# Modulation weights loaded in tiles of 512 columns, and two modulation steps moved from the second expert stage into the second mixer

## The chip, the cores and the metric

The kernel runs on one core of one Trainium2 chip. The core has five engines that run their own instruction streams: TensorE (PE in the profile; its weight loads are listed apart as PEld), VectorE (DVE), ScalarE (ACT), GpSimd (POOL) and SyncE (SP), which here only issues transfers. Sixteen DMA engines move data between device memory and the core's on-chip memory. The metric is the time of one execution on the device, in microseconds.

## The reference

A diffusion-transformer block of two layers over 256 latent tokens and 256 context tokens, width 1024, batch 1, all in float32. Each layer has a mixer and a mixture of experts, and both are modulated by vectors that are made from the conditioning vectors c (for the latent tokens) and c_ctx (for the context):

```python
mod_lat = jnp.split((jax.nn.silu(c) @ w_mod[l] + b_mod[l])[:, None, :], 6, axis=-1)
mod_ctx = jnp.split(jax.nn.silu(c_ctx) @ w_mod[l] + b_mod[l], 6, axis=-1)
u_lat = to_scan_order(rms_norm(h_lat, norm1_g[l]) * (1 + mod_lat[1]) + mod_lat[0], rows, l)
...
z_lat = jnp.split(u_lat @ w_in[l], split_at, axis=-1)
...
y_lat = from_scan_order(jnp.concatenate([a_lat, m_lat, r_lat], axis=-1) @ w_out[l], rows, l)
h_lat = h_lat + mod_lat[2] * y_lat
v_lat = rms_norm(h_lat, norm2_g[l]) * (1 + mod_lat[4]) + mod_lat[3]
h_lat = h_lat + mod_lat[5] * hier_moe(v_lat, *moe_p)
```

`w_mod[l]` is 1024 x 6144. The mixer (`a`, `m`, `r`) is a gated convolution of 31 taps, a chunked mLSTM with four heads in two directions, and a gated linear recurrence. `hier_moe` routes each token to 2 of 16 experts (width 512; three matrices of 1024 x 512 each). In the last layer only the latent tokens go through the convolution, the output projection and the experts. The result is a final RMS norm of the latent tokens.

## The kernel before

The program runs mixer, experts, mixer, experts. PE's order is the order in which the code is written (a manual schedule for PE); the orders of ACT, DVE, POOL and SP and the use of the buffers are chosen by the framework's scheduler, from the dependences and its own model of the program.

**Modulation.** The 6144 columns of a layer are worked off in twelve steps q = 0 to 11 of 512 columns (two steps to one of the six vectors). A step loads its 2 MB of `w_mod` as two tiles (`wcols`, L209 to L210, whose transfers are recorded at L187). `mod_mm` (L219 to L230) multiplies them with `cS`, the silu of both conditioning vectors, spread over groups of 32 output partitions (L225), and copies the sum to `mp` (L228, ACT). `mod_fin` transposes `mp` four times on PE (L234), adds the four partial sums on DVE (L236) and the bias (L238), into `modc`. Whoever needs a vector reads `modc`. Between the two halves of a step the next one may start: `pump` places `mod_mm` of the next step and then `mod_fin` of the one before it, on PE behind the place where it is called. In the mixers these places have names (`site("k1")` and so on), and the table `SITES` says at which of them a step is placed; `pump(100)` at the end of the mixer's heads takes what is left. In the expert stages `pump(2)` is called twice ahead of the routing, and again at places of the last expert of the first layer.

**Where the steps stand.** Layer 1's first six steps are done in the first expert stage, steps 6 to 9 in the second mixer at k1, v3, g0 and o0, and steps 10 and 11 at the start of the second expert stage. Steps 10 and 11 make `mod_lat[5]`, which `gate_rows` reads when the fourth expert of the order is worked off (`OVER`).

**Buffers.** A ring of seven tiles of 1 MB holds weights of `w_in`, `w_out` and `w_mod`, and in the expert stages also expert weights. A tile of `w_in` or `w_out` is split into a high and a low part (`wsplit`): ACT casts the high part (L191), DVE and POOL each subtract one half of it from the raw tile (L192), so that it takes three tiles of the ring. Expert weights (`ahead`, `ewt`; transfers at L1122 and L1128) go into fifteen buffers in turn: B, three pairs of q4 halves, uLa, uLb, the ring, uTa and uTb. Most of these are also buffers of the second mixer, and a load waits until the mixer has given its buffer back. SP issues all loads in one order.

**The second mixer.** After the projections of q, k, v (L517) the mLSTM goes through its chunks (`chunk_b`); in a chunk PE multiplies `X`, the masked and scaled scores, with the values (L837) and the scaled queries `qs` with the state (L839). DVE makes `X` in steps (L813, L814, L822), POOL makes `qs` (L821), and DVE reads the normaliser `dn` (L840) and adds the heads' outputs into `hacc` (L865). The convolution's norm (L911 to L931) and the recurrence's gate `g` (POOL L953, L954; DVE L955, L957) run beside it. Then come the two tiles of the output gate (`o_tile`, L517, with two tiles of `w_in`, the o-weights), the heads' norm (L985 to L998), and `w_out` (L1050).

**The start of the second expert stage.** Behind `w_out` DVE makes `xs`, the normalised tokens (L275); PE transposes them (L283) and multiplies with the router's weights (L331); DVE makes the routing from the logits (L1177 to L1311, `m`); PE then sorts (L1218 to L1259), and the first expert's gate and up projections begin (L1356).

Of the kernel before, what the change touches and what calls it, by code (L numbers as in the profile page):

```python
# [14 lines left out]
P = 128  # L15
D = 1024
KC = 8
# [10 lines left out]
NPE = 1  # L28
BP = (2, 3)

SITES = ("q0 q1 k0 v3 v1 o0 o1", "k1 v3 g0 o0")
PV = ((1, 1), (1, 1))
START = {mybir.EngineType.Activation, mybir.EngineType.DVE, mybir.EngineType.Pool, mybir.EngineType.SP}
LOE = ((0, 1), (0, 1), (0, 1), (0, 1))
# [5 lines left out]
def hybrid_kernel(ctx, tc, x, c, cx, c_ctx, w_mod, b_mod, norm1_g, norm2_g, w_in, conv_w, conv_b, conv_ln_g,  # L40
# [4 lines left out]
    V, S, G, T = nc.vector, nc.scalar, nc.gpsimd, nc.tensor  # L45
# [13 lines left out]
    def bank(shape=(P, 512)):  # L59
        cnt[0] += 1  # L60
        return box["ps"].tile(list(shape), F32, tag="ps", name=f"ps{cnt[0]}", bufs=box["nps"])

    def kt(shape, dt=F32, name=None, tag=None, bufs=1):
        return keep.tile(list(shape), dt, name=name, tag=tag or name, bufs=bufs)
# [68 lines left out]
    cS = kt([P, KC, 32], name="cS")  # L133
# [50 lines left out]
    def wtile(src, shape, pool=None):  # L184
        wn[0] += 1
        t = (pool or ring).tile(list(shape), F32, tag="w", name=f"w{wn[0]}")
        nc.sync.dma_start(t, src)  # L187
        return t
# [20 lines left out]
    def wcols(w, a, n=256):  # L209
        return wtile(w[:, a:a + n].rearrange("(k p) f -> p k f", p=P), [P, KC, n])  # L210


    def mod_ld(l, q, between=None):
        a = wcols(w_mod[l], q * 512)
        if between:
            between()
        return [a, wcols(w_mod[l], q * 512 + 256)]

    def mod_mm(l, q, tmp, ws=None):  # L219
        ps = bank()  # L220
        for hf in range(2):
            w = ws[hf] if ws else wcols(w_mod[l], q * 512 + hf * 256)
            for k in range(KC):
                j = k % 4
                T.matmul(ps[32 * j:32 * j + 32, hf * 256:hf * 256 + 256], cS[:, k, :], w[:, k, :],  # L225
                         start=(k < 4), stop=(k >= 4))
        mp = tmp.tile([P, 512], F32, tag="t2", name=f"mp{l}_{q}")
        S.copy(mp, ps)  # L228
        return mp
# [10 lines left out]
    def mod_pair(l, q, tmp):  # L240
        mod_fin(l, q, mod_mm(l, q, tmp))
# [108 lines left out]
    def mixer(l, hs, fill):  # L350
# [5 lines left out]
        with tc.tile_pool(name=f"mx{l}", bufs=1, reuse_waits="tile") as mx, \  # L356
# [23 lines left out]
            def pump(n=1):  # L380
                for _ in range(n):
                    late = box.pop("late", None)
                    if fill:
                        box["late"] = fill.pop(0)(tmp)
                    if late:
                        late()

            def site(name):
                pump(SITES[l].split().count(name))

# [15 lines left out]
            if l == 0:  # L406
# [8 lines left out]
                warm = sm("warm", [P, 1])  # L415
                S.activation(warm, onec, AF.Silu)
                mw = {0: mod_ld(0, 0)}
                xin = [hload(x, "xl", "hl"), hload(cx, "xc", "B")]
                mw[2] = mod_ld(0, 2)
                w16 = thin_w()  # L420

# [7 lines left out]
                for q in (1, 3):  # L429
                    mw[q] = mod_ld(0, q)  # L430
# [36 lines left out]
                def warm_up(n):  # L467

                    for _ in range(n):
                        T.matmul(wps[:, 0:P], ident, ident, start=True, stop=True)  # L470

                mp0 = mod_mm(0, 0, tmp, mw[0])
                columns(1)
                mod_fin(0, 0, mp0)
# [3 lines left out]
                into(1)  # L478
                turn((0, 1))
                mp2 = mod_mm(0, 2, tmp, mw[2])  # L480
                warm_up(3)
                w0 = [wx[1:]]
# [1240 lines left out]
    def mod_late(l, q, tmp):  # L1723
        mp = mod_mm(l, q, tmp)

        def fin():
            mod_fin(l, q, mp)
            if (l, q) == (1, 3):
                mod_scale(s1, 1, 1, "n1")
        return fin  # L1730

    mods = [[(lambda tmp, l=l, q=q: mod_late(l, q, tmp)) for q in range(12)] for l in range(2)]
    with tc.manual_schedule(engines={mybir.EngineType.PE}):
        hs = mixer(0, None, mods[0][4:])
        hs = moe(0, hs, mods[1][:4 + len(BP)])
        hs = mixer(1, hs, mods[1][4 + len(BP):10])
        moe(1, hs, mods[1][10:])


_INS = ['x', 'c', 'ctx', 'c_ctx', 'w_mod', 'b_mod', 'norm1_g', 'norm2_g', 'w_in', 'conv_w', 'conv_b', 'conv_ln_g',  # L1740
# [49 lines left out]
```

## Time and profile before

| | |
|---|---|
| median of 3 runs | 1188.36 us (1186.65 to 1193.46) |
| profiled execution | 1189.1 us, its span 1187.5 us |
| busy share of the span | PE 88%, DVE 46%, ACT 31%, POOL 19% |
| moved by DMA | 313.19 MB, mean 264 GB/s |
| loads of w_mod | 48 of 1024 KB, median 6.8 us from issue to landing |

The span is the time from the first to the last instruction of the profiled execution; the whole execution takes a little longer. All times of single instructions are counted from the start of the span. A matmul of the program appears as two or more records in the trace. The names of the ring's tiles are left out in the trace (`w`), while the split tiles keep theirs (`w238h` for a high part, `w238l` for a low part).

### The profile page before, as it was taken

The numbers are of one execution on the slowest core, as the hardware profiler recorded it, in microseconds if no ns is written. First come the engines' busy times: TensorE is split into PE (matmuls) and PEld (weight loads), VectorE is DVE, ScalarE is ACT, GpSimd is POOL, SyncE is SP. The second block draws the span as 40 slices with busy tenths as digits, with TensorE's granted clock in tenths as the row PEclk, the third lists the DMA queues.
The fourth block names the chain that finished last, engine by engine and source line by source line (L and its number), as shares of the span: only waits on it lengthen the run. The fifth ranks groups of instructions, "written<-read, shape, count | busy, mean of one in ns | idle before, by whom it ended". The sixth has DMA issues, their size and how long they took to land. (4 is left out here: it accounts for less than half of the span.)

```text
span 1187.5 us, 21557 instructions
## 1 busy us (share of the span) xinstructions
PE 1040.2 (88%) x8655; PEld 718.5 (61%) x8655; DVE 541.1 (46%) x1239; ACT 363.4 (31%) x713; POOL 227.7 (19%) x241
## 2 busy tenths in 40 slices
PE   6989989999989979999999678989887887888966
PEld 4667778899764535445453356769786564455532
DVE  3779977762451111120101789974775211012115
ACT  3545254443331111111111344644442221122202
POOL 3412123414100000000000634111441000000112
PEclk9999989999999989999999889989998998999998
DMA  9735743376878877898887633442679899999981
GB/s 314 228 106 169 258 145 96 107 252 245 261 312 336 324 256 310 308 369 333 341 324 289 217 120 109 142 142 95 222 271 381 330 411 412 412 406 412 412 317 54
DMA packets 144009, 313.19 MB, mean 264 GB/s; under 512 B 26116, under 2 KB 108336, under 8 KB 124032
## 3 DMA queue, kind: packets, MB, share of 16 engines
q1 hardware_dynamic: 128896, 295.74, 67.4%
q0 software_dynamic: 14704, 14.92, 3.9%
q8 instruction: 102, 1.67, 0.6%
q10 hardware_dynamic: 272, 0.57, 0.1%
q14 instruction: 35, 0.29, 0.1%
HBM read 298.25 MB, written 20.71 MB: 269 GB/s over the span
## 5 line engine op out<-in xcount | busy, mean ns | idle before, releaser
L1391 DVE TENSOR_TENSOR hT<-sg,ps 128x256 f32<-128x256 f32 x63 | 24.9, 421 | 319.7 <-ACT sg L1382 319.3
L1356 PE MATMUL X<-w,XT 128*32 128x256 f32 (+1 forms) x2016 | 138.1, 398 | 22.9 <-PEq L1647 6.4
L1472 POOL DMA_DIRECT2D Yd<-Y x90 | 33.4, 386 | 518.9 <-ACT Y L1468 462.8
L1356 PEld LDWEIGHTS X<-w,XT 128*32 128x32 f32 (+1 forms) x2016 | 75.7, 113 | 84.1 <-issue 38.4
L1356 PE MATMUL ps<-w,XT 128*64 128x512 f32 x512 | 115.9, 605 | 11.3 <-PEq L1478 5.9
L1242 PE MATMUL ps<-P,vh 128*128 128x256 f32 x336 | 87.7, 297 | 9.5 <-PEq L1611 8.1
L1356 PEld LDWEIGHTS ps<-w,XT 128*64 128x64 f32 x512 | 42.9, 139 | 80.5 <-issue 64.7
L1242 PE MATMUL ps<-P,vl 128*128 128x256 f32 x336 | 82.7, 282 | 0.0
L756 DVE SCALAR_TENSOR_TENSOR acc<-cb,cwh,acc 128x512 f32<-128x512 f32 (+1 forms) x120 | 80.1, 706 | 1.0
L1242 PEld LDWEIGHTS ps<-P,vh 128*128 128x128 f32 x336 | 64.2, 191 | 24.5 <-issue 12.1
L1373 ACT COPY gs<-X 128x512 f32<-128x512 f32 x45 | 26.3, 586 | 169.3 <-PEq L1611 55.5
L1468 DVE COPY Y<-Y 128x512 f32<-128x512 f32 x30 | 20.8, 692 | 98.3 <-PEq L1647 29.4
L1404 PE MATMUL Y<-w,hT 128*32 128x256 f32 (+1 forms) x912 | 59.7, 387 | 5.6 <-issue 4.0
L1242 PEld LDWEIGHTS ps<-P,vl 128*128 128x128 f32 x336 | 64.3, 191 | 0.0
L225 PE MATMUL ps<-w,cS 128*32 128x256 f32 x768 | 49.6, 397 | 10.1 <-DMA w<-in_w_mod_dram 9.7
L1404 PE MATMUL ps<-w,hT 128*64 128x512 f32 x240 | 54.8, 598 | 0.3 <-DVE hT L1391 0.2
L1379 PE MATMUL ps<-blob,gs 128*128 128x128 f32 x256 | 42.0, 290 | 10.8 <-PEq L1624 3.4
L1404 PEld LDWEIGHTS Y<-w,hT 128*32 128x32 f32 (+1 forms) x912 | 28.7, 111 | 33.6 <-issue 14.7
L1373 ACT COPY gs<-ps 128x512 f32<-128x512 f32 x15 | 8.8, 587 | 123.6 <-PE ps L1356 123.6
L1379 PEld LDWEIGHTS ps<-blob,gs 128*128 128x128 f32 x256 | 27.7, 144 | 26.7 <-issue 15.5
L225 PEld LDWEIGHTS ps<-w,cS 128*32 128x32 f32 x768 | 22.7, 113 | 31.1 <-DMA w<-in_w_mod_dram 11.0
L1382 ACT ACTIVATE sg<-ps 128x256 f32<-128x256 f32 x64 | 24.2, 391 | 43.4 <-PE ps L1379 26.8
(893 smaller groups left out, 2083.3 us busy)
## 6 DMA issues: line engine op xcount, KB each, us to landing
w<-in_w_down_dram SPq DMA_DIRECT2D x58, 1024.0 KB, 13.0
w<-in_w_gate_dram SPq DMA_DIRECT2D x49, 1024.0 KB, 11.3
w<-in_w_mod_dram SPq DMA_DIRECT2D x48, 1024.0 KB, 6.8
w<-in_w_up_dram SPq DMA_DIRECT2D x48, 1024.0 KB, 12.2
w<-in_w_in_dram SPq DMA_DIRECT2D x23, 1024.0 KB, 6.6
w<-in_w_up_dram SPq DMA_DIRECT2D x32, 512.0 KB, 9.1
w<-in_w_gate_dram SPq DMA_DIRECT2D x30, 512.0 KB, 10.0
w<-in_w_out_dram SPq DMA_DIRECT2D x8, 1024.0 KB, 5.5
```

The costliest lines, as they stand in the source:

```text
L225: T.matmul(ps[32 * j:32 * j + 32, hf * 256:hf * 256 + 256], cS[:, k, :], w[:, k, :], start=(k < 4), stop=(k >= 4))
L756: V.scalar_tensor_tensor(acc[:, ch], src, wcol, acc[:, ch], op0=OP.mult, op1=OP.add)
L1242: T.matmul(ps[:, cc, :], v[:, i, k * P:k * P + P], P2[:, i, :], start=(n == 0), stop=(n == 2 * NT - 1))
L1356: T.matmul(ps[w * t:w * t + w, o0:o0 + q], XT[:, k, c0:c0 + w], ws[2 * g + k // 4][k % 4][:, f0:f0 + q], start=(k == 0), stop=(k == KC - 1))
L1373: S.copy(o, src)
L1379: T.transpose(pt[:, f, :], gs[:, f * P:f * P + P], ident)
L1382: S.activation(sg, pt[:, :, 0:64], AF.Silu)
L1391: V.tensor_tensor(hT, sg, pt[:, :, 64:128], op=OP.mult)
L1404: T.matmul(ps[w * t:w * t + w, o0:o0 + q], hk, ws[4 + k // 2][k % 2][:, q * t:q * t + q], start=(k == 0), stop=(k == 3))
L1468: (V.tensor_copy if b else S.copy)(Y, ps)
L1472: nc.gpsimd.dma_start(Yd[x, s0:s0 + w, :].rearrange("s (h f) -> h s f", f=q), Y[:, q * c:q * c + q], **({"cond": n_s > s0} if s0 else {}))
```

## The change

Each load of a modulation step takes 512 rows and all of the step's 512 columns, where before it took all 1024 rows and 256 columns; the tile is 128 x 4 x 512 instead of 128 x 8 x 256. A step's matmuls have 512 columns and there are eight instead of sixteen. `SITES[1]` has two more places, v2 and g1; the second mixer is given steps 6 to 11, and the second expert stage none. Behind the edited functions line numbers fall by 3 or 4.

```diff
-SITES = ("q0 q1 k0 v3 v1 o0 o1", "k1 v3 g0 o0")
+SITES = ("q0 q1 k0 v3 v1 o0 o1", "k1 v2 v3 g0 g1 o0")
...
-    def mod_ld(l, q, between=None):
-        a = wcols(w_mod[l], q * 512)
-        if between:
-            between()
-        return [a, wcols(w_mod[l], q * 512 + 256)]
+    def mod_ld(l, q):
+        return [wtile(w_mod[l][512 * h:512 * h + 512, q * 512:q * 512 + 512].rearrange("(k p) f -> p k f", p=P),
+                      [P, 4, 512]) for h in range(2)]
 
     def mod_mm(l, q, tmp, ws=None):
         ps = bank()
-        for hf in range(2):
-            w = ws[hf] if ws else wcols(w_mod[l], q * 512 + hf * 256)
-            for k in range(KC):
-                j = k % 4
-                T.matmul(ps[32 * j:32 * j + 32, hf * 256:hf * 256 + 256], cS[:, k, :], w[:, k, :],
-                         start=(k < 4), stop=(k >= 4))
+        ws = ws or mod_ld(l, q)
+        for k in range(KC):
+            j = k % 4
+            T.matmul(ps[32 * j:32 * j + 32, :], cS[:, k, :], ws[k // 4][:, j, :], start=(k < 4), stop=(k >= 4))
...
-        hs = mixer(1, hs, mods[1][4 + len(BP):10])
-        moe(1, hs, mods[1][10:])
+        hs = mixer(1, hs, mods[1][4 + len(BP):])
+        moe(1, hs, [])
```

On SP, in the second mixer, before (the last two `w_in` tiles are the o-weights; 128x1024 are halves of expert weights in q4 buffers):

```order
L187 DMA w_8991<-in_w_mod_dram 128x8x256
L1128 DMA w_9713<-in_w_gate_dram 128x2048
L187 DMA w_9001<-in_w_mod_dram 128x8x256
L187 DMA w_9168<-in_w_in_dram 128x8x256
L187 DMA w_9176<-in_w_in_dram 128x8x256
L1122 DMA w_9715<-in_w_up_dram 128x1024
L187 DMA w_9318<-in_w_mod_dram 128x8x256
L187 DMA w_9328<-in_w_mod_dram 128x8x256
L187 DMA w_9446<-in_w_out_dram 128x8x256
```

And the same place after the change:

```order
L187 DMA w_8853<-in_w_mod_dram 128x4x512
L1124 DMA w_9581<-in_w_gate_dram 128x2048
L187 DMA w_8855<-in_w_mod_dram 128x4x512
L187 DMA w_9023<-in_w_mod_dram 128x4x512
L187 DMA w_9025<-in_w_mod_dram 128x4x512
L187 DMA w_9044<-in_w_in_dram 128x8x256
L1118 DMA w_9583<-in_w_up_dram 128x1024
L1118 DMA w_9584<-in_w_up_dram 128x1024
L1118 DMA w_9587<-in_w_gate_dram 128x1024
L1118 DMA w_9588<-in_w_gate_dram 128x1024
L187 DMA w_9052<-in_w_in_dram 128x8x256
```

One more step's tiles stand ahead of the o-weights, and four halves of expert weights now stand between the two o-weights.

On DVE, at the last chunk of the mLSTM, before (`w240l` is the low part of the second o-weight, `X` and `dn` belong to the chunk, `g` to the recurrence's gate, `xnat` to the convolution's norm):

```order
L822 TENSOR_TENSOR X_9080<-X_9080,st_1_8827 128x512
L814 TENSOR_TENSOR X_9080<-X_9080,blob 128x512
L916 BN_AGGR bag_8942<-bst_8941 128x2
L192 TENSOR_TENSOR w240l<-w_9176,w240h 128x1024
L822 TENSOR_TENSOR X_9080<-X_9080,st_0_8820 128x512
L917 TENSOR_SCALAR bag_8942<-bag_8942 128x1
L840 COPY dn_3_0_9184<-ps_9185 128x2
L840 COPY dn_3_0_9184<-ps_9191 128x2
L919 TENSOR_SCALAR xnat_8940<-ps_9116,bag_8942 128x256
L915 BN_STATS bst_8941<-ps_9116 128x6
L955 SCALAR_TENSOR_TENSOR g_9157<-g_9157,g_9156 128x256
```

And after (`w242l` is the low part of the first o-weight; that of the second, `w244l`, comes later, behind the sums into `hacc`):

```order
L818 TENSOR_TENSOR X_8934<-X_8934,st_1_8689 128x512
L810 TENSOR_TENSOR X_8934<-X_8934,blob 128x512
L912 BN_AGGR bag_8804<-bst_8803 128x2
L913 TENSOR_SCALAR bag_8804<-bag_8804 128x1
L915 TENSOR_SCALAR xnat_8802<-ps_8970,bag_8804 128x256
L911 BN_STATS bst_8803<-ps_8970 128x6
L951 SCALAR_TENSOR_TENSOR g_9011<-g_9011,g_9010 128x256
L818 TENSOR_TENSOR X_8934<-X_8934,st_0_8682 128x512
L912 BN_AGGR bag_8804<-bst_8803 128x2
L232 TENSOR_REDUCE modc_80<-ps_9037 128x8
L913 TENSOR_SCALAR bag_8804<-bag_8804 128x1
L192 TENSOR_TENSOR w242l<-w_9044,w242h 128x1024
```

The last multiplication of `X` now stands behind `xnat` and `g`, and the splits of the o-weights stand behind it instead of ahead of it.

On PE, from the last projection of the gate `g` to the last chunk, before:

```order
L507 MATMUL ps_9131<-ul1a,w234h 128x256 x4
L507 MATMUL ps_9131<-ul1b,w234h 128x256 x4
L837 MATMUL ps_9185<-va_8498,X_9080 128x129
L839 MATMUL ps_9185<-C_8501,qs_9081 128x129
L837 MATMUL ps_9185<-va_8498,X_9080 128x129
```

And after:

```order
L503 MATMUL ps_8985<-ul1a,w236h 128x256 x4
L503 MATMUL ps_8985<-ul1b,w236h 128x256 x4
L222 MATMUL ps_9022<-w_9023,cS 32x512 x4
L222 MATMUL ps_9022<-w_9025,cS 32x512 x4
L230 MATMUL ps_9037<-blob,mp_9_8865 128x128 x4
L833 MATMUL ps_9061<-va_8346,X_8934 128x129
L835 MATMUL ps_9061<-C_8349,qs_8935 128x129
```

A modulation step (place g1) now stands between the projection and the chunk; one such step more stands at v2, among the projections of q, k, v, and two fewer stand behind `w_out`.

## Rows read from the trace of the kernel before

**Rows 1.** Stretches: length, busy PE, PEld, DVE, ACT, POOL, clock, DMA share, GB/s.

```profile
788.00:796.00 8.00, 2.93 (x14) 2.94 (x15) 5.46 (x11) 4.45 (x6) 1.92 (x1) 0.76 1.08 353
844.00:852.00 8.00, 5.36 (x42) 4.83 (x41) 7.89 (x18) 6.19 (x17) 4.37 (x3) 1.00 0.64 202
908.00:916.00 8.00, 3.11 (x18) 2.42 (x17) 5.38 (x42) 0.78 (x3) 0.00 (x0) 0.73 1.00 415
924.00:932.00 8.00, 6.52 (x84) 4.50 (x80) 1.77 (x6) 3.60 (x6) 0.00 (x0) 1.00 0.45 168
1004.00:1012.00 8.00, 7.07 (x105) 4.26 (x103) 2.94 (x8) 1.08 (x3) 0.73 (x3) 1.00 1.01 415
```

**Rows 2.** SP's queue in the second mixer and after (start, length, line, transfer).

```profile
827.81 7.05 SPq L187 DMA_DIRECT2D w<-in_w_in_dram  x2
...
887.54 6.79 SPq L187 DMA_DIRECT2D w<-in_w_mod_dram  x4
...
928.01 0.33 SPq L1128 DMA_DIRECT2D w<-in_w_up_dram  x1
```

**Rows 3.** The page's group of the modulation matmuls: busy, mean ns, idle before, releaser.

```profile
L225 PE MATMUL ps<-w,cS 128*32 128x256 f32 x768 | 49.6, 397 | 10.1 <-DMA w<-in_w_mod_dram 9.7
```

**Rows 4.** PE's timeline where modulation steps wait (start, length, idle before, releaser).

```profile
314.45 1.07 PE L225 MATMUL ps<-w,cS 128*32 128x256 f32 x16 [1.98 <-DMA w<-in_w_mod_dram]
...
327.95 1.07 PE L225 MATMUL ps<-w,cS 128*32 128x256 f32 x16 [1.15 <-DMA w<-in_w_mod_dram]
...
700.90 1.07 PE L225 MATMUL ps<-w,cS 128*32 128x256 f32 x16 [1.74 <-DMA w<-in_w_mod_dram]
```

**Rows 5.** PE's timeline at the end of the second mixer.

```profile
853.62 0.72 PE L517 MATMUL ps<-w238h,uh1a 128*128 128x256 f32 x4
...
859.70 1.93 PE L225 MATMUL ps<-w,cS 128*32 128x256 f32 x32
861.56 0.66 PE L234 MATMUL ps<-blob,mp 128*128 128x128 f32 x4
861.98 0.71 PE L517 MATMUL ps<-w238h,uh1a 128*128 128x256 f32 x4
...
870.88 1.11 PE L234 MATMUL ps<-blob,mp 128*128 128x128 f32 x4 [2.31 <-ACT mp L228]
...
878.28 0.74 PE L1050 MATMUL ps<-w244h,mixMh 128*128 128x256 f32 x4 [1.14 <-ACT mixMh L191]
```

**Rows 6.** PE's timeline, gate logits with 512 columns at the second mixer's start.

```profile
716.93 1.06 PE L331 MATMUL ps<-uh1a,w 128*32 128x512 f32 x8
717.81 1.04 PE L331 MATMUL ps<-uh1b,w 128*32 128x512 f32 x8
```

**Rows 7.** DVE's timeline around the last chunk of the second mixer.

```profile
835.38 0.43 DVE L955 SCALAR_TENSOR_TENSOR g<-g,g 128x256 f32<-128x256 f32 x1 [4.90 <-POOL g L954]
...
847.81 2.20 DVE L192 TENSOR_TENSOR w240l<-w,w240h 128x1024 fp32r<-128x1024 f32 x1
849.94 1.75 DVE L822 TENSOR_TENSOR X<-X,st 128x512 f32<-128x512 f32 x1
...
853.52 2.50 DVE L955 SCALAR_TENSOR_TENSOR g<-g,g 128x256 f32<-128x256 f32 x1
...
868.62 1.20 DVE L192 TENSOR_TENSOR w244l<-w,w244h 128x1024 fp32r<-128x1024 f32 x1
```

**Rows 8.** POOL's timeline around the last chunk of the second mixer.

```profile
852.64 0.74 POOL L954 TENSOR_TENSOR g<-g,g 128x256 f32<-128x256 f32 x1
853.32 2.41 POOL L192 TENSOR_TENSOR w240l<-w,w240h 128x1024 fp32r<-128x1024 f32 x1
```

**Rows 9.** Timelines of PE and DVE at the start of the second expert stage.

```profile
903.23 1.07 PE L225 MATMUL ps<-w,cS 128*32 128x256 f32 x16 [1.34 <-DMA w<-in_w_mod_dram]
...
903.27 1.42 DVE L275 TENSOR_SCALAR xs<-hn,sq 128x1024 f32<-128x1024 f32 x2 [0.18 <-POOL sq L270]
...
914.31 0.61 PE L1218 MATMUL ps<-AA,blob 128*128 128x32 f32 x2 [4.43 <-DVE m L1303]
```

## The prediction

> **What bounds the kernel now.** I read the busy shares first, then the engines in stretches of 8 us, and only then the order of single instructions on the four engines where the change moves something. The busy shares of the whole span say little here: they are means over stages with different limits, and the change touches three of these, so each is read by itself.
>
> In the second mixer PE and DVE take turns. From 844 to 852 us DVE is busy for 7.89 of 8 us while PE is busy for 5.36 [rows 1]: there DVE sets the pace, and work added to PE can be covered, while work moved on DVE cannot. In the expert stage that follows the DMA engines set it: in 1004 to 1012 they move 415 GB/s [rows 1] for engines that wait for weights. One hole is in that stream: in 924 to 932 only 168 GB/s move [rows 1]. The transfer queue has then nothing it may start: every prefetch buffer is full, and the next load is issued at 928.01 [rows 2], when the first expert's matmuls have given buffer B back. From there the weights that are left are a fixed amount, and the end of the kernel shifts with the moment at which this load goes out.
>
> The modulation steps themselves are 24 times 32 matmul records (768), 49.6 us of PE, and the idle time directly ahead of them is 10.1 us, of which the loads of w_mod ended 9.7 [rows 3]. So faster loads have at most 9.7 us to give, all stages together.
>
> **Part 1: loads of 512 columns, eight matmuls for sixteen.** A step's loads stay two tiles of 1 MB (2.10 MB in all); a contiguous run in DRAM grows from 1 KB to 2 KB. In 788 to 796, when nothing but tiles of 256 columns moves, the rate is 353 GB/s; in 1004 to 1012, expert weights in runs of 8 KB, it is 415 [rows 1]. One tile takes 1.049 MB / 353 = 2.97 us by the one and 2.53 us by the other. Runs of 2 KB don't occur in a stretch of their own, so the gain per tile is bounded by 0 and 0.44 us; between the two ends I take 0.24, about the middle. Where does it count? At three places in the steady part PE waits for the last tile of a group of steps: 1.98 us at 314.45, 1.15 us at 327.95, 1.74 us at 700.90 [rows 4]. Behind the first two the first expert stage's routing is queued, behind the third the second mixer's first projection. Two steps' loads stand ahead of each wait, four tiles, but part of them sits in the ring already; I count two or three tiles, 0.6 us per wait at the first expert stage (1.2) and 0.4 at the mixer, and 0.7 for the waits at the start of the kernel, which are most of what is left of the 9.7. That is 2.3 us. Bounds: 0, if the run length changes nothing, and 4 tiles x 0.44 x 4 groups = 7.0.
>
> The Trainium skill has a rule that speaks against this part: its page "DMA: Bandwidth & Descriptors", Specifications, gives 512 B as the smallest transfer for the full line rate, so that 1 KB would be no worse than 2 KB or 8 KB. By that rule the sum would lose its 2.3 us. The trace has 353 against 415 GB/s where the rule has no difference, and so I keep the gain.
>
> On PE a step's 32 records take 1.86 us from start to start (859.70 to 861.56), and its four transposes 0.42 more (to 861.98) [rows 5]. Eight records of 32 x 512 with another operand take 0.88 us (716.93 to 717.81 [rows 6]), so that sixteen take 1.76: 0.10 less a step. It is small, and I use it only below.
>
> **Part 2: two steps moved into the second mixer.** Each brings 1.76 + 0.42 = 2.18 us of PE, one copy on ACT and two small operations on DVE; what leaves the expert stage is the same. Three costs follow.
>
> The step at v2 stands in the stretch in which PE does the q, k, v projections back to back. It adds 2.18, less 0.1 for each of the two or three steps already there: +1.9 us at the chunk that follows. The step at g1 stands on PE just ahead of the last chunk, where DVE sets the pace and PE has 8 - 5.36 = 2.64 us to spare [rows 1]; I count it at nothing, and at 2.18 if that cover is gone.
>
> The second cost is the order that comes with it. On DVE the last multiplication that makes the last chunk's X ran at 849.94 for 1.75 us, right after the split of an o-weight (847.81, 2.20 us), done at 851.69 [rows 7]. It now comes behind the operation on g (853.52 before), which waits for POOL: the g that it needs was ready at 852.64 + 0.74 = 853.38 [rows 8]. With the 1.9 us from v2 that is 855.3; then 0.43 for g, as at 835.38 [rows 7], and 0.68 for an X alone: 856.4, some 4 to 4.7 us later than before. PE's last chunk waits for it. The two splits of the o-weights that DVE did before this point now come after it, the second behind all the sums of heads that need the last chunk. The output gate's first tile began on PE at 853.62 [rows 5] with all its weights; now its second half waits for that split. Adding up DVE's operations from X to the split in the new order by their old durations (7.9 us, then 0.4 of statistics and 1.2 to 2.2 for the split itself) gives 866 to 867, and PE has 1.8 us of matmuls after it: the tile ends at about 868. Before, the step behind it began at 859.70 [rows 5], so this is some 8 us later, and the second tile follows it.
>
> The third is what takes it back. Ahead of w_out PE waited 2.31 us at 870.88 and 1.14 us at 878.28 [rows 5], for ACT and the mixer's normalised heads. Up to 3.45 us of the 8 vanish in these; but the splits of w_out also sit behind the new last step on POOL and DVE, and return about one. I take +5.5 us at the end of the mixer. Bounds: +1.9, if only v2's matmuls count, and +10.7, worked out under the rivals. Its weights are no part of it: the second o-weight is loaded behind four halves of expert weights now, where both went out by 834.9 [rows 2]. The halves are freed by the chunk before the last, and DVE had done with that one when it began the split at 847.81 [rows 7]; even from there the halves (2.1 MB) and the tile take 3.15 MB / 353 = 8.9 us, so it lands by 857, nine before DVE wants it.
>
> In the expert stage four tiles of w_mod, 4.2 MB, no longer load (they went out from 887.54 on [rows 2]), and the two steps no longer run ahead of the router. Their last matmuls ended at 904.3, after a wait of 1.34 us; but the transposes behind them also waited for DVE's xs, made from 903.27 to 904.69 [rows 9]. So the steps were nearly covered, and taking them away brings 0 to 0.3 us. PE now stands idle there from the end of w_out to 904.69, and then again for 4.43 us at 914.31 [rows 9]. Around the second of these, which is there already, the granted clock is 0.73 in 908 to 916 [rows 1], a mean of time at 2.4 GHz and time at 1.2. I add 0.6 us for more records at the lower level; bounds are -0.3 and, for 4 us of matmuls at 0.73 of the clock, 4 / 0.73 - 4 = +1.5.
>
> **Sum.** The profiled execution took 1189.1 us, 0.7 over the median of the three runs. 1189.1 - 2.3 + 5.5 + 0.6 = 1192.9 by its clock, and 1192.2 against the median: **1192 us**. All lower bounds together give 1188.4 - 7.0 + 1.9 - 0.3 = 1183, all upper ones 1188.4 + 10.7 + 1.5 = 1200.6; they will hardly meet, and for this case I take the inner half, 1187 to 1197.
>
> **Rivals.**
> *The stream of expert weights ends earlier.* Four tiles less at 415 GB/s are 10.1 us; if the stage is bound by transfers from 887 on, the end comes that much sooner: 1188.4 - 10.1 = 1178. For it: 415 GB/s in 1004 to 1012. Against it: the hole in 924 to 932, which only becomes longer when the buffers are full sooner.
> *DVE and POOL stand in each other's way (slower).* At 853.52 DVE's operation on g took 2.50 us where it takes 0.43 at 835.38 [rows 7]; POOL's half of an o-weight's split ran from 853.32 to 855.73 [rows 8]. It decides if in the new order X, g and both splits each fall beside a POOL operation: X 1.75 for 0.68, g 2.50 for 0.43, two splits of 2.20 for 1.20 (868.62 [rows 7]). That is 1.1 + 2.1 + 2.0 = 5.2 us on DVE's chain to the output gate: +10.7 in place of +5.5, 1197 us. The Trainium skill's page "SBUF — State Buffer", Who interferes with whom, has a rule for it: DVE and GpSimd share a pair of ports as a lock that one holds for a whole instruction. Here the trace agrees, since the operation ended 0.3 us after POOL's did. Against this rival: in the new order g comes ahead of the splits, and need not meet them.
> *The steps are hidden.* PE's and DVE's idle places of the second mixer take the two steps and the order, and the loads alone count: 1188.4 - 2.3 = 1186. For it: PE waits of 3.45 us ahead of w_out, and 2.64 us in 844 to 852. Against it: X now stands behind a wait for POOL.
> *The wide loads bring nothing,* and the rest is as forecast: 1194.5. For it: a good part of the 9.7 us may be the fixed time from issue to landing, which a run's length doesn't change.
>
> **How the numbers follow.** Forecast 0.50 (1187 to 1197), contention 0.20 (1197), steps hidden 0.13 (1186), loads bring nothing 0.08 (1194.5), shorter stream 0.09 (1178). Half a per cent, about what a measurement of this kernel can tell from no change, is 5.9 us: 1182.4 to 1194.3. Slower takes the contention, half of the loads' case and a fifth of the forecast's: 0.34. Faster takes the shorter stream and a little of the hidden steps: 0.11. The rest, 0.55, is within. The range 1180 to 1199 leaves out the shorter stream and the far end of the contention, somewhat under 2 in 10.
>
> **What would show it.** In the new profile the records of the modulation steps number 384 instead of 768, and the idle time ahead of them is near 7 us. In the second mixer the last chunk's X ends 4 to 5 us later counted from the mixer's first projection, the first output-gate tile ends 8 us later, w_out ends 5 to 6 us later; from there to the end of the kernel the distance stays, with the hole in the transfers longer than before. I am wrong if the distance from the first expert's matmuls to the end shrinks by several us (the stream), if the first output-gate tile ends on time (my order of DVE's work), or if X and g show 1.7 and 2.5 us again (contention).

## The result and the profile after

The changed kernel takes 1198.3 us (median of six runs, 1196.68 to 1201.84), the kernel before 1189.65 us beside it. The ratio is 1.0068 with a 95% interval of 1.0051 to 1.0086: slower by 0.7%, some 8 us. The profiled execution has a span of 1195.7 us against 1187.5.

Where the 8 us arise is read by marks in PE's timeline that both programs have. The columns are the start of the second mixer's first projection, then, counted from it, the last matmul pair of the last chunk, the start of `w_out` and its end, and last the time from `w_out`'s end to the first expert's matmuls (all us). The other rows are the kernels of the experiments below.

| kernel | first projection | last chunk | w_out starts | w_out ends | to first expert |
|---|---|---|---|---|---|
| before | 703.7 | 149.5 | 169.6 | 195.5 | 23.7 |
| changed | 701.5 | 154.3 | 174.7 | 204.1 | 25.6 |
| wide loads only | 704.0 | 155.0 | 172.0 | 201.9 | 23.7 |
| move only | 704.7 | 155.1 | 176.2 | 203.6 | 25.6 |
| changed, PE kept busy | 701.7 | 155.1 | 175.7 | 203.0 | 22.5 |
| X first, loads and places of before | 704.4 | 151.1 | 167.6 | 198.0 | 24.1 |
| X first, wide loads | 700.8 | 150.4 | 167.0 | 197.5 | 23.9 |
| X first, wide loads and move | 702.0 | 160.1 | 176.5 | 205.1 | 25.2 |
| 18 steps wide, PE kept busy | 702.3 | 150.6 | 168.8 | 197.4 | 22.5 |
| two steps behind the router, wide loads | 703.6 | 154.8 | 171.6 | 201.6 | 24.1 |
| ACT's order, changed | 704.0 | 152.9 | 172.5 | 202.5 | 25.6 |
| ACT's order, wide loads | 704.1 | 154.2 | 171.5 | 201.5 | 23.8 |
| ACT's order, loads and places of before | 701.7 | 153.0 | 170.6 | 197.6 | 24.1 |
| ACT's order, wide loads, PE kept busy | 701.2 | 153.0 | 170.0 | 200.4 | 22.5 |

The first column must be read with care: the four profiled kernels with the old loads have it between 701.7 and 704.7 (mean 703.6), though they are the same program up to there. The columns counted from the mark repeat better, but not to the tenth: the changed kernel and its copy with PE kept busy have the same second mixer (204.1 and 203.0), and so have the kernel before and the one with 18 wide steps, with the same order on every engine (195.5 and 197.4). So up to 2 us in the column of `w_out`'s end show nothing. The last column, the stage behind `w_out`, is the steadiest: three kernels with PE kept busy all have 22.5.

The second mixer is 8.7 us longer, the start of the second expert stage 1.9 us. From the first expert to the end nothing more comes: its matmuls start at 931.27 instead of 922.86, 8.4 us later, and the spans differ by 8.2.

PE's timeline of the changed kernel (start, length, line, operation, in brackets the idle time ahead and what ended it); rows 4, 5 and 9 of before answer to it:

```profile
698.72 1.06 PE L222 MATMUL ps<-w,cS 128*32 128x512 f32 x8 [1.48 <-DMA w<-in_w_mod_dram]
...
854.15 0.49 PE L833 MATMUL ps<-va,X 128*128 128x129 f32 x2 [3.56 <-DVE X L818]
...
856.53 1.21 PE L513 MATMUL ps<-w242h,uh1a 128*128 128x256 f32 x4
...
863.45 0.72 PE L513 MATMUL ps<-w244l,uh1a 128*128 128x256 f32 x4 [1.99 <-DVE w244l L192]
...
867.56 1.06 PE L222 MATMUL ps<-w,cS 128*32 128x512 f32 x8 [0.59 <-DMA w<-in_w_mod_dram]
...
868.96 0.71 PE L513 MATMUL ps<-w242h,uh1a 128*128 128x256 f32 x4
...
877.59 0.51 PE L1046 MATMUL ps<-w248l,mixOh 128*128 128x256 f32 x2 [0.47 <-POOL w248l L192]
...
881.63 0.73 PE L1046 MATMUL ps<-w248h,mixMh 128*128 128x256 f32 x4 [1.13 <-ACT mixMh L191]
...
884.08 0.74 PE L1046 MATMUL ps<-w248h,mixMl 128*128 128x256 f32 x4 [1.24 <-DVE mixMl L192]
...
893.82 0.50 PE L1046 MATMUL ps<-w252l,mixOh 128*128 128x256 f32 x2 [1.27 <-POOL w252l L192]
...
900.43 0.50 PE L1046 MATMUL ps<-w254l,mixOh 128*128 128x256 f32 x2 [0.72 <-POOL w254l L192]
...
910.65 4.04 PE L279 MATMUL ps<-blob,xs 128*128 128x128 f32 x16 [5.02 <-DVE xs L271]
...
922.72 0.61 PE L1214 MATMUL ps<-AA,blob 128*128 128x32 f32 x2 [4.87 <-DVE m L1299]
...
931.27 3.66 PE L1352 MATMUL X<-w,XT 128*32 128x256 f32 x64
```

The last chunk waits 3.56 us for X. The first output-gate tile starts at 856.53, 2.9 us later than before, and its second half waits 1.99 us for `w244l`; the second tile starts at 868.96 instead of 861.98 [rows 5], 7 us late. Some of this is caught up ahead of `w_out`, and lost again within it, to POOL's splits of the third and fourth tile (893.82, 900.43), waits that before doesn't have. Before waits there for `mixMh` [rows 5] and, less long, for `mixMl`:

```profile
880.17 0.74 PE L1050 MATMUL ps<-w244h,mixMl 128*128 128x256 f32 x4 [0.67 <-DVE mixMl L192]
```

DVE and POOL around the last chunk of the changed kernel:

```profile
846.22 1.77 DVE L810 TENSOR_TENSOR X<-X,blob 128x512 f32<-128x512 f32 x1
...
851.05 2.44 DVE L951 SCALAR_TENSOR_TENSOR g<-g,g 128x256 f32<-128x256 f32 x1
...
853.42 0.68 DVE L818 TENSOR_TENSOR X<-X,st 128x512 f32<-128x512 f32 x1
...
861.43 1.97 DVE L192 TENSOR_TENSOR w244l<-w,w244h 128x1024 fp32r<-128x1024 f32 x1
```

```profile
850.17 0.75 POOL L950 TENSOR_TENSOR g<-g,g 128x256 f32<-128x256 f32 x1
850.85 2.36 POOL L192 TENSOR_TENSOR w242l<-w,w242h 128x1024 fp32r<-128x1024 f32 x1
...
859.94 2.37 POOL L192 TENSOR_TENSOR w244l<-w,w244h 128x1024 fp32r<-128x1024 f32 x1 [4.00 <-DMA w<-in_w_up_dram]
```

The operation on g began at 851.05 beside POOL's split of `w242l`, which ran from 850.85 to 853.21, and took 2.44 us; X, which stands behind it, followed at 853.42. Before, the same collision was there [rows 7, 8], but behind X. The queue and the stretches of the changed kernel:

```profile
828.11 3.09 SPq L187 DMA_DIRECT2D w<-in_w_mod_dram  x3
...
845.46 0.38 SPq L187 DMA_DIRECT2D w<-in_w_in_dram  x1
...
926.40 0.33 SPq L1124 DMA_DIRECT2D w<-in_w_up_dram  x1
...
936.43 0.33 SPq L1124 DMA_DIRECT2D w<-in_w_up_dram  x1
```

```profile
316.00:318.00 2.00, 2.00 (x20) 2.00 (x19) 2.00 (x5) 2.00 (x5) 0.00 (x0) 1.00 1.04 386
911.00:919.00 8.00, 6.27 (x34) 4.15 (x33) 3.35 (x11) 2.67 (x6) 0.00 (x0) 0.64 0.30 125
919.00:926.00 7.00, 3.28 (x16) 3.31 (x17) 5.89 (x42) 1.41 (x4) 0.00 (x0) 0.59 0.01 4
```

The columns are those of rows 1. The first stretch holds w_mod loads of 2 KB runs at 386 GB/s; the same stretch of before, with 1 KB runs, has 349:

```profile
316.00:318.00 2.00, 2.00 (x21) 2.00 (x19) 1.18 (x4) 1.59 (x5) 0.00 (x0) 1.00 1.09 349
```

In 919 to 926 hardly a byte moves, and in 911 to 919 little: a hole of some 14 us, up to the load at 926.40, now stands ahead of the one that before has in 924 to 932 [rows 1]. The load that ends before's hole at 928.01 [rows 2] goes out at 936.43 here, 8.4 us later, as much as the first expert's matmuls. The clock is granted at 0.64 in 911 to 919, behind 5.02 us in which PE was idle, and at 0.59 in 919 to 926, most of it the lower of its two levels (1.2 GHz), with another 4.87 ahead of the sorting at 922.72. The transposes of `xs` show what that costs: 4.04 us at 910.65, where before's take 1.91:

```profile
904.72 1.91 PE L283 MATMUL ps<-blob,xs 128*128 128x128 f32 x16
```

The page's group of the modulation matmuls has half as many records and 2.9 us less idle time than in rows 3:

```profile
L222 PE MATMUL ps<-w,cS 128*32 128x512 f32 x384 | 48.5, 618 | 7.2 <-DMA w<-in_w_mod_dram 6.9
```

### The profile page after: what moved, and what is told of

The parts are those of the page before. It is cut to its first block, busy times and chain, and to the rows that moved or that the text cites. A ratio compares the mean times of both kernels' runs of the same rounds, so it can differ in the third digit from the quotient of the medians.

```text
span 1195.7 us, 20788 instructions
## 1 busy us (share of the span) xinstructions
PE 1042.2 (87%) x8271; PEld 707.5 (59%) x8271; DVE 542.1 (45%) x1239; ACT 363.4 (30%) x713; POOL 223.0 (19%) x241
## 5 line engine op out<-in xcount | busy, mean ns | idle before, releaser
L222 PE MATMUL ps<-w,cS 128*32 128x512 f32 x384 | 48.5, 618 | 7.2 <-DMA w<-in_w_mod_dram 6.9
L1400 PEld LDWEIGHTS ps<-w,hT 128*64 128x64 f32 x240 | 15.9, 136 | 28.2 <-issue 25.1
```

The source lines that it names most:

```text
L222: T.matmul(ps[32 * j:32 * j + 32, :], cS[:, k, :], ws[k // 4][:, j, :], start=(k < 4), stop=(k >= 4))
L1400: T.matmul(ps[w * t:w * t + w, o0:o0 + q], hk, ws[4 + k // 2][k % 2][:, q * t:q * t + q], start=(k == 0), stop=(k == 3))
```

## The experiments

Each ratio is to the kernel before on the same chip, with its 95% interval.

**The parts apart.** The wide loads with the old places:

```diff
-SITES = ("q0 q1 k0 v3 v1 o0 o1", "k1 v2 v3 g0 g1 o0")
+SITES = ("q0 q1 k0 v3 v1 o0 o1", "k1 v3 g0 o0")
...
-        hs = mixer(1, hs, mods[1][4 + len(BP):])
-        moe(1, hs, [])
+        hs = mixer(1, hs, mods[1][4 + len(BP):10])
+        moe(1, hs, mods[1][10:])
```

Expected: 

> Only the wide loads and the 512-column matmuls; the steps stand where they stood before. Theory (the move costs, the loads give): the waits ahead of the steps fall by about 2 us up to the second mixer, as in the changed kernel (703.70 to 701.51 at its first projection), part of it is lost to the first w_in split, so 0.5 to 2 us faster than before, about 1187.5 to 1189; at the first expert's matmuls no more than 1 us from before's 922.9. Rival (the wide loads themselves delay the second mixer, by the ring or the order they bring): 4 us or more slower than before, w_out's end past 903.

Measured: 1.0032 (1.0016 to 1.0048), slower. The rival was nearer: the second mixer is 6.4 us longer than before without any step moved. Its ACT, DVE, POOL and SP orders had changed. They are the scheduler's choice, and around the last chunk it had chosen for X and g what it chose for the changed kernel: X behind g, g beside POOL's split.

```profile
853.13 2.44 DVE L951 SCALAR_TENSOR_TENSOR g<-g,g 128x256 f32<-128x256 f32 x1
...
855.49 0.68 DVE L818 TENSOR_TENSOR X<-X,st 128x512 f32<-128x512 f32 x1
```

```profile
856.32 0.77 PE L833 MATMUL ps<-va,X 128*128 128x129 f32 x2 [4.91 <-DVE bag L912]
...
900.73 0.50 PE L1046 MATMUL ps<-w250l,mixOh 128*128 128x256 f32 x2 [1.15 <-POOL w250l L192]
```

PE waits 4.91 us at 856.32. The trace names DVE's `bag` as what ended it; that is the small operation right behind X (855.49 + 0.68 = 856.17), so it is X that PE waited for. Of the 6.4 us 2.4 are there when `w_out` starts; 4.0 come within it, from more waits (4.0 us in all, for 1.8 before) and from slower matmuls, at a granted clock of 0.94 for 0.98 (the stretch of `w_out`, here and then before):

```profile
876.03:905.91 29.88, 25.86 (x203) 24.85 (x205) 12.08 (x14) 10.72 (x22) 13.64 (x7) 0.94 0.72 253
```

```profile
873.35:899.16 25.81, 24.00 (x202) 23.42 (x204) 11.07 (x14) 9.57 (x21) 14.07 (x6) 0.98 0.80 275
```

The move with the old loads, from the kernel before with the new `SITES` and lists. Expected: 

> Only the move of the two steps, with loads of 256 columns. Theory: all of the loss comes from the move, and the gain of the loads is missing: 8.5 to 11 us slower than before, w_out's end 6.5 to 9 us later than before's 899.2. Rival (half of the loss comes from the loads): 3 to 5 us slower.

Measured: 1.0075 (1.0055 to 1.0095), about 9 us, with the end of `w_out` 9.2 us later than before's in its profile. As expected in size. But with the run before it, the parts are +0.32% and +0.75%, and both together +0.68%: they don't add up. Either alone has X behind g in its trace, which a second edit can't cost again.

**The clock at the start of the second expert stage.** At the two places there where PE waits:

```diff
             pump(2)
+            if last:
+                filler()
             vT = pair("uT", f"vT{l}")
...
             flush()
+            if last:
+                filler()
```

with `filler` sixteen matmuls of 512 columns on constants. Expected: 

> The changed kernel plus sixteen matmuls of 512 columns on constants at each of the two places at the start of the second expert stage where PE waits (for xs, and for the routing m); their results are not used. Theory (the clock falls to 1.2 GHz in the idle time, and the transposes, router, sorting run at it): the granted clock of the sorting's stretch rises from 0.50 towards 1, from w_out's end to the first expert's matmuls it takes 22 to 24 us instead of 25.7, and the run is 1.5 to 3 us faster than the changed kernel. Rival (that stage is set by DVE's routing and ACT, not by the clock): the stretch stays within 0.5 us of 25.7, no gain.

Measured: 1.0050 (1.0032 to 1.0068). The stage takes 22.5 us instead of 25.6, with the same loads and the same work on DVE; the granted clock (third column from the right) is 1.00 from the transposes to the first expert where the changed kernel has 0.64 and 0.75:

```profile
909.70:919.80 10.10, 8.07 (x66) 3.47 (x66) 6.77 (x37) 2.72 (x7) 0.00 (x0) 1.00 0.24 99
919.80:927.20 7.40, 6.70 (x52) 6.24 (x52) 6.72 (x33) 2.64 (x5) 0.00 (x0) 1.00 0.56 211
```

```profile
910.60:922.70 12.10, 6.62 (x34) 4.35 (x35) 7.07 (x37) 3.04 (x7) 0.00 (x0) 0.64 0.23 93
922.70:931.20 8.50, 8.39 (x52) 8.14 (x52) 7.16 (x34) 2.93 (x5) 0.00 (x0) 0.75 0.44 162
```

The time moved the way the theory says, by 0.18%; since the two intervals overlap, the stage's 3.1 us in the traces are the firmer number.

Then, with wide loads, the two steps behind the router instead of these matmuls: the first `pump(2)` left out in the last layer, the second one kept. Expected: 

> Wide loads; steps 6 to 9 in the second mixer as before, steps 10 and 11 in the second expert stage but behind the router instead of ahead of it, in PE's wait for the routing. Theory: PE has 4.4 us of idle time there, the two steps take 3.6 to 4.5 and keep the clock up for the sorting; the second mixer is as before: 1 to 4 us faster than before, 1186 to 1188.5. Rival (the steps are late for want of their loads or push the sorting back): 0 to 4 us slower than before.

Measured: 1.0041 (1.0026 to 1.0056). The expectation failed, as its second mixer is not "as before": it has the order of the wide loads alone (201.6 us). The stage itself takes 24.1 us, no better than before's 23.7: the sorting behind the steps runs at a granted clock of 1.00, but ahead of the router PE is now idle for 5.02 us, and the transposes there take 4.03 us where before's take 1.91.

**The order of the last chunk.** First only ACT's order, in the changed kernel, in the wide loads alone and in the kernel before:

```diff
-            chunk_a(3)
-            ln_in()
-            lru_gate(1)
-            site("g1")
+            with tc.manual_schedule(engines={mybir.EngineType.PE, mybir.EngineType.Activation} if last else {mybir.EngineType.PE}):
+                chunk_a(3)
+                ln_in()
+                lru_gate(1)
+                site("g1")
```

Expected, changed kernel: 

> The changed kernel, and in the second mixer ACT's operations of the last chunk's first half, of the convolution's norm and of the gate g in the order in which the code is written, so that X's second exponential no longer stands behind a cast of the o-weight, and DVE's last multiplication of X stands ahead of xnat and g again. Theory (the loss of the second mixer is this order, which both edits bring alike, and not the two steps): PE's last chunk starts 2 us or more earlier than in the changed kernel, w_out ends at 900 to 903.5 instead of 905.6, the run is 2 to 5 us faster than the changed kernel. Rival (the two steps themselves, their loads and the ring cost it): within 1 us of the changed kernel.

Expected, wide loads: 

> Only the wide loads, with the steps where they stood before, and with the same order of ACT in the second mixer. Theory: w_out ends within 1.5 us of before's 899.2 instead of 905.9, 4 to 7 us faster than the wide loads alone, which is 0 to 3 us faster than before. Rival (the wide loads cost by themselves): 2 us or more slower than before.

Expected, before: 

> The kernel before with the same order of ACT in the second mixer: a control for the order alone. X stands ahead of xnat and g there already. Theory: within 1.5 us of before. Rival (the written order is better than any of the others by itself): 3 us or more faster than before, and then the gains of the other runs with it are not the order of X.

Measured: 1.0043 (1.0026 to 1.0061), 1.0026 (1.0013 to 1.0039) and 1.0014 (0.9998 to 1.0031). X did come ahead of g, and little was won: 154.2 us to the last chunk with wide loads instead of 155.0. The changed kernel reaches it at 152.9 instead of 154.3, and its `w_out` ends at 906.5, not at the 900 to 903.5 that was expected; its ratio is lower by the forecast amount, but the two intervals overlap. With wide loads the new order had put POOL's split of the o-weight between the two qs, and X now met that:

```profile
849.34 2.20 DVE L192 TENSOR_TENSOR w240l<-w,w240h 128x1024 fp32r<-128x1024 f32 x1
...
851.88 2.41 DVE L818 TENSOR_TENSOR X<-X,st 128x512 f32<-128x512 f32 x1
```

```profile
850.41 3.33 POOL L192 TENSOR_TENSOR w240l<-w,w240h 128x1024 fp32r<-128x1024 f32 x1
...
854.67 1.28 POOL L817 TENSOR_TENSOR qs<-qs,qT 128x512 f32<-128x512 f32 x1
```

X takes 2.41 us for 0.68, and the last qs is ready only at 855.95. So this was no clean test. The control failed too: with the loads and places of before, this order reaches the last chunk at 153.0 us instead of 149.5.

The wide loads with ACT's order and the filler at the second place only. Expected: 

> As the run before last (wide loads, steps where they stood, ACT's order), plus sixteen matmuls on constants, whose result is not used, in PE's wait for the routing of the second expert stage. Theory: the sorting runs at 2.4 GHz, 1 to 1.5 us less from the start of the sorting to the first expert, so 1 to 4.5 us faster than before, and the fastest of all. Rival: the stage ends by DVE, no faster than the kernel without these matmuls.

Measured: 1.0000 (0.9982 to 1.0017). From the sorting to the first expert it takes 7.4 us, where the same kernel without these matmuls takes 8.7; not faster than before, with the mixer still at 200.4.

Then the whole end of the chunk written out for ACT, DVE and POOL, so that no split can stand beside X:

```diff
+                for d in range(2):
+                    G.tensor_tensor(qs2[:, d], qs2[:, d], qT[:, :, ii[d] * P:ii[d] * P + P], op=OP.mult)
...
+                stats(0)
+                V.tensor_tensor(X2_[:, 0], X2_[:, 0], STs[ii[0]], op=OP.mult)
+                stats(1)
+                V.tensor_tensor(X2_[:, 1], X2_[:, 1], STs[ii[1]], op=OP.mult)
...
+                G.tensor_tensor(g2[:, :NO], g2[:, :NO], g1[:, :NO], op=OP.mult)
+                wos.append(wsplit(w_in[l], 2304))
...
+                wos = [wsplit(w_in[l], 2048)]
+                E = mybir.EngineType
+                with tc.manual_schedule(engines={E.PE, E.Activation, E.DVE, E.Pool}):
+                    tail()
```

Expected, before: 

> The kernel before with the last chunk's end written out for ACT, DVE and POOL: both exponentials and multiplications of X and both qs first, then the convolution's norm, then the split of the second o-weight, then g. No POOL split can fall beside X. Theory (what decides the second mixer is which DVE operations meet a POOL split, and so the order): PE's last chunk starts at or up to 2 us ahead of before's place (147 to 149.6 us after the mixer's first projection, where before has 149.6), the run within 2 us of before. Rival (order doesn't decide): as before's other order run, 152 us and more.

Expected, wide loads: 

> The wide loads alone, with the same written-out order. Theory: the last chunk starts 147 to 150.5 us after the mixer's first projection instead of 155.0, w_out ends 3 us or more earlier than in the wide loads alone, and the run is 2 to 5 us faster than the wide loads alone. Rival (the wide loads cost by themselves, whatever the order, say because w_out's tiles then come late from the ring): within 1.5 us of the wide loads alone, still 2 us or more slower than before, with PE's waits for POOL's split of w_out still there.

Expected, changed kernel: 

> The changed kernel (wide loads and the move) with the same written-out order; the two o-weights' loads then stand together again. Theory: the last chunk starts 148.5 to 152 us after the mixer's first projection instead of 154.3, the run is 2 to 5 us faster than the changed kernel; against the run before this one it shows what the two added steps cost by themselves, 2 to 4 us with the cold clock at the start of the second expert stage. Rival (the steps and their loads cost it all): within 1.5 us of the changed kernel.

Measured: 1.0007 (0.9994 to 1.0021), 1.0003 (0.9989 to 1.0016) and 1.0059 (1.0039 to 1.0079). This is the square of loads and places with one order. The wide loads alone go from +0.32% to no difference, and their second mixer from 201.9 to 197.5 us, with X at its place:

```profile
846.85 1.02 DVE L1002 TENSOR_TENSOR X<-X,st 128x512 f32<-128x512 f32 x1
...
847.87 1.21 DVE L192 TENSOR_TENSOR w240l<-w,w240h 128x1024 fp32r<-128x1024 f32 x1
```

```profile
846.34 0.46 PE L833 MATMUL ps<-va,X 128*128 128x129 f32 x2 [2.22 <-DVE X L1000]
...
886.40 0.50 PE L1112 MATMUL ps<-w248l,mixOh 128*128 128x256 f32 x2 [1.14 <-POOL w248l L192]
```

X still takes 1.02 for 0.68 us, beside qs. So what the wide loads cost was the order: with one order for both, the kernels with and without them can't be told apart. That X is the part of the order that counts is less clear. Up to `w_out`'s start this order wins 2.6 us on the kernel before, and 2.0 with the old loads; in both this is lost within `w_out`, to waits such as that for POOL's split (1.14 us at 886.40): it takes 30.5 and 30.4 us there, and 25.9 before. The changed kernel did not follow: its expectation failed, and the rival's "within 1.5 us of the changed kernel" came true. With X first it is still 0.6% slower. X is done 150.2 us after the first projection, and PE comes to the last pair of the chunk only at 160.1, because it waits for something else:

```profile
852.88 1.93 PE L222 MATMUL ps<-w,cS 128*32 128x512 f32 x8 [4.48 <-DMA w<-in_w_mod_dram]
...
855.97 1.93 PE L222 MATMUL ps<-w,cS 128*32 128x512 f32 x8 [1.15 <-DMA w<-in_w_mod_dram]
```

```profile
829.53 0.37 SPq L187 DMA_DIRECT2D w<-in_w_in_dram  x1
...
847.49 1.32 SPq L187 DMA_DIRECT2D w<-in_w_mod_dram  x2
```

The step at g1 waits 4.48 and 1.15 us for its weights. The two o-weights' loads stand together again (from 829.53 on), and the step's two tiles, which in the changed kernel go out in the three issues from 828.11 on, go out behind them, at 847.49 and 848.43; the queue waits 5.0 us for the projection of the gate g to give a tile back. A split o-weight takes three tiles of the ring, two of them six of its seven, and a step takes two. So with the move one of them goes out late: here the step, and in the changed kernel the second o-weight (845.46, where before has both out by 834.9 [rows 2]), for whose landing no engine waits there.

**The wide loads without a new order.** Wide loads in the first eighteen steps, where the scheduler's order of the second mixer comes out as that of before, and the filler at the second place:

```diff
     def mod_mm(l, q, tmp, ws=None):
         ps = bank()
+        if (l, q) < (1, 6) and not ws:
+            ws = [wtile(w_mod[l][512 * h:512 * h + 512, q * 512:q * 512 + 512].rearrange("(k p) f -> p k f", p=P),
+                        [P, 4, 512]) for h in range(2)]
...
```

Expected: 

> The kernel before with wide loads and 512-column matmuls in the first eighteen steps only (up to the end of the first expert stage); the six steps of the second mixer and second expert stage keep their tiles of 256 columns and their places, and with them every engine's order in the second mixer is that of before. At the start of the second expert stage the sixteen matmuls on constants in PE's wait for the routing are added, their result is not used. Theory: the second mixer takes 195 to 197 us from its first projection to w_out's end, as before's 195.5 (the wide loads alone had 201.9); the first projection comes 1 to 3 us earlier than in before; from w_out's end to the first expert 22.3 to 22.8 instead of 23.7. In sum 1 to 4 us faster than before. Rival (the wide loads lengthen the second mixer whatever its order): 200 us or more in the mixer, not faster than before.

Measured: 0.9989 (0.9975 to 1.0003), which can't be told from no change. The mixer takes 197.4 us, 0.4 over the theory and clear of the 200 of the rival; the stage behind it 22.5, as expected. Of all kernels this has the lowest ratio, but none beats the kernel before clearly.

## Why the prediction was right, and where it was wrong

It forecast 1192 us, in a range of 1180 to 1199. 1198.3 lies in the range, close to its end: the kernel became 8.65 us slower, where 3.8 were forecast, and slower by more than half a per cent had a chance of 0.34, less than the 0.55 for no such change. In the two profiles the parts are -2.2 us up to the second mixer, +8.7 in it, +1.9 in the stage behind it and -0.2 from there on; the forecast has -2.3, +5.5, +0.6 and nothing. Of its signs, X ends 4.6 us later counted from the first projection (4 to 5), the first output-gate tile 8.4 (8), `w_out` 8.7 (5 to 6). Direction and place are right; too small are what `w_out` gives back and the clock.

*The loads (-2.3 us).* Right in the rate: 386 GB/s between 349 and 415, 0.29 us a tile by these against the 0.24 taken. The waits ahead of the steps fell by 2.8 us (9.7 to 6.9). What arrives is smaller: ten profiles with wide loads in the first eighteen steps reach the second mixer at 702.5 on average, four without at 703.6, so some 1 us, less than the spread of either group. In the changed kernel's profile 2.2 us were won by then (the wait at its start is 1.48 for 1.74) and 0.75 were left at the modulation step behind the k projections (783.78 for 784.53), where the splits of `w_in` and DVE set the pace. With the order held there is no measurable gain (1.0003). That the loads could cost something was in no term: the prediction took it that they change nothing but transfers and matmuls. This is the step that failed. Alone they made the kernel 0.32% slower, by the order that the scheduler built on them.

*The step at v2 (+1.9).* Right at the chunk that follows: from 0.75 us early, the changed kernel is 1.1 us late at the first state update (813.32 for 812.23). It doesn't last to the end of the mLSTM, as the next point shows.

*The order of the last chunk.* Right in kind: X behind g, the second o-weight's split behind the heads, the first gate tile's second half waiting for it. That X ends just where it was forecast, 152.6 us after the first projection, is luck: two errors cancel. The forecast has POOL's g ready 1.9 us later than before and g taking 0.43 us. POOL's g was ready at 850.92 (850.17 + 0.75), counted from the first projection 0.3 us earlier than before, probably because the split of the first o-weight, which before stands ahead of that point, now stands behind it; and g took 2.44 us beside POOL's split. X behind g was laid to the move alone; it comes with either edit.

*What `w_out` returns (+1).* Mis-sized. At its start the kernel is 2.8 us late by the spans' clock (876.17 for 873.35), where the forecast's terms give 2.2; at its end 6.5, so 3.7 are given back and not one. The waits for POOL's splits and `mixMl` within it are 3.0 us longer than before. For the third tile this is not the load: it had landed at 885.43, and ACT casts it only at 889.19, behind its operations on yt, which wait for POOL:

```profile
888.38 0.42 ACT L1061 ACTIVATE yt<-hn 128x256 f32<-128x256 f32 x1 [6.80 <-POOL hn L1059]
...
889.19 1.98 ACT L191 CAST w252h<-w 128x1024 fp32r<-128x1024 f32 x2
```

*The clock (+0.6, up to 1.5).* Mis-sized. The stage became 1.9 us longer, beyond its bound. The bound took 4 us of matmuls at 0.73 of the clock, which is a mean of both levels; the transposes ran at the lower one, 4.04 us for 1.91, and DVE's routing waits for them and the router. The time from the sorting to the first expert is the same as before (8.55 us, at a granted clock of 0.75). The matmuls on constants took back 3.1 us, more than was lost, because they sped up the sorting too.

*The rivals.* The shorter stream (0.09) is refuted: 4.2 MB less, and the hole of the transfers became longer by about as much. Contention (0.20) happened, with 2.44, 1.77 and 1.97 us where 0.43, 0.68 and 1.2 are enough, 3.9 us in all; but before has 4.1 us of the same [rows 7]. It was not more of it, it stood ahead of X: of its sign, g showed 2.44 us again, and the last X 0.68. The steps were not hidden, and the loads brought nothing on the whole.

What stays open: how much of the last 0.6% with X first is the ring and how much the two steps' own work, which a ring of more tiles would tell; it wasn't tried. How much of the order's cost is X behind g and how much the order within `w_out` was not parted either. And why the scheduler's own model flips the order on a tile's shape.

## What to carry to other kernels

Where a scheduler sets the order, an edit that saves a little on one engine can reorder others far away: compare the orders of all engines first, at the stage that is tightest, and time each part alone, since two parts that bring the same bad order don't add up. Work that is moved into a stage needs buffers there as well as time: count the ring's tiles that are held at once. And a stage with a small dependent matmul chain pays for idle time ahead of it by the clock; keeping PE busy took 1.2 to 3.1 us off that stage in the traces, though no kernel became clearly faster than the one before by it.

## What the runs showed of the hardware

A DVE operation that reads two SBUF tensors and starts beside a POOL operation that does so too ends behind it, by not quite its own length: 0.28 us behind POOL's split for a g of 0.43 us, 0.55 behind a split or a qs for an X of 0.68, 1.09 behind a split for one of 1.20. So g took 2.44 us and X 2.41; the delay is what is left of POOL's operation (2.36 to 3.33 us). Loads of 1 MB tiles moved 349 and 386 GB/s with runs of 1 and 2 KB, in the same stretch of 2 us, and 415 with runs of 8 KB in another stage. With PE kept busy by matmuls whose result is not used, the granted clock stayed at 1.00 through a stage in which it was 0.64 and 0.75.
